# A mixer and mixture-of-experts trunk: a ninth slot for expert weights, a weight ring of ten, and a new order at the start, in the router and in the tail

## The chip, the cores and the metric

The kernel runs on one core of a Trainium2 chip. The metric is the time of one execution in microseconds (us), less is better. A core has four engines with an instruction stream each, TensorE (PE), VectorE (DVE), ScalarE (ACT) and GpSimd (POOL), and SyncE (SP), whose stream here holds almost nothing but transfers from and to memory. Each engine runs its stream in order and waits at an instruction until what it needs is done.

## The reference, cut to what matters

One layer on 256 tokens of width 2048; everything in float32.

```
mod = silu(c) @ ada_w + ada_b                     # six vectors of 2048: sh1, sc1, g1, sh2, sc2, g2
h = rmsnorm(x) * (1 + sc1) + sh1
proj = h @ mix_in_w                               # q, k, v of 16 heads, and u of 4 Fourier groups
y_na = neighborhood_attention(q, k, v, rpb) @ na_out_w
y_f = fourier_mix(u) @ fourier_out_w
g_na, g_f = split(sigmoid(h @ branch_gate_w + b))
x = x + g1 * ((g_na * y_na + g_f * y_f) @ mix_out_w)
h = rmsnorm(x) * (1 + sc2) + sh2
group = argmax(h @ router_group_w + b);  two best of its 8 experts by h @ router_expert_w + b
x = x + g2 * sum over the two of weight * (silu(h @ w_gate) * (h @ w_up)) @ w_down
out = rmsnorm(x) * final_g
```

The weights of all 32 experts are read: each has a gate and an up matrix of 2048x512 and a down matrix of 512x2048.

## The kernel before, in words

**Split products.** The projections keep float32's accuracy by splitting: a weight chunk of 128x1024 numbers (half a MB) is loaded by `load` (line 103) into a ring of eight slots, ScalarE rounds it to `hi` (line 107), VectorE takes `lo = w - hi` (line 108), and TensorE adds three products, hi with hi, hi with lo and lo with hi, into PSUM (`t_part`, `n_part`; all matmuls come from `mm`, line 116). The activations are split in the same way, into `hh` and `hl` (mixer) or `mh` and `ml`.

**Start and mixer, up to about 545 us.** c is spread over the partitions (`condR`, line 197). x comes in as two tiles of 128 tokens, `xt[0]` and `xt[1]`; ScalarE squares and sums them (line 339), VectorE scales both by 1/rms (line 342), TensorE transposes, and the eight pieces of `xT` are copied out of PSUM by VectorE and ScalarE in turn (line 350). The modulation of the first norm (sh1, sc1) comes from 64 chunks of `ada`, for which VectorE does one multiply with a sum each (`dot`, line 215). Eight such dots make the modulation `ab` of two of the sixteen 128-channel blocks of x; `h_pair` then forms `hf` (block one on VectorE, line 252, block two on ScalarE, line 253) and splits it into hh and hl. Only then can TensorE use those two blocks. The first pass over the input weights (`mixw`, `gatew`) goes by four such steps of two pairs each; in each step nine outputs take two chunks of weights. The other modulations (`ada`, 128 chunks) are macs on VectorE (line 223), one after most chunks of the mixer. A scheduler that estimates when each operand is ready sets the order of each engine's stream there.

**The stage of mow, about 545 to 641.7 us.** 4 column blocks of 512 with 8 chunks of `mix_out_w` each. `residual` (lines 600 to 602) multiplies by g1, adds to x1 and squares; `router_part` transposes x1 (line 610) and multiplies it with the router's weights (`plg`). SyncE's order is as the program text has it: beside the 32 mow chunks, 20 quarters (half a MB each) of the first five expert chunks (`early_some`, line 572) and 14 ada chunks; 9 ada chunks are loaded behind the last mow chunk (`late`), and their macs are called behind `gather(0)`.

**Transition.** The logits, with the 36 outputs on partitions, are copied (`lgs`, line 647), turned by a selector matmul and scaled to `lg` (line 656); then come the two best experts, their ranks `rk`, and `gather(0)`: selection matrices `gt`, gathered tokens `ph`, `hq`.

**The experts.** Eight quads of four experts with up to 32 tokens each. A quad reads 24 chunks `exw` of 128x4096 numbers: 16 for gate and up (`pg`, `pu`), 8 for down (`pd`, then `po` back to the tokens and a sum into x2). SyncE issues each chunk (line 727) as soon as its slot is free; there are seven slots in a ring and an eighth used once. The last quad ends with a norm and the output (`tail`, lines 886 to 918). A value `nri` that says whether a token list has over 32 entries goes to SyncE (line 869), and a loop runs only if so.

## Time and profile before

| | |
|---|---|
| median of 3 runs | 1600.57 us (1597.12 to 1603.39) |
| the profiled execution | 1598.41 us, its span 1596.6 us |
| bytes moved | 616.27 MB |
| TensorE busy | 1233.2 us, 77% of the span |
| VectorE busy | 679.3 us, 43% |
| ScalarE busy | 349.7 us, 22% |

The span runs from the first to the last instruction of the profiled execution; starts in the rows are counted from it. "Busy" counts an engine's instructions, however well they are packed. The transfers are run by 16 engines of their own, whose share and rate (GB/s) the profile gives for any stretch. PEclk is the clock that TensorE was granted, as a part of full speed.

### The profile page before, as it was taken

What the parts mean: (1) busy time and instruction counts of PE and PEld (TensorE: products, weight loads), DVE (VectorE), ACT (ScalarE), POOL (GpSimd) and SP (SyncE); (2) the same over time, 40 slices, a digit from 0 to 9 for tenths busy, and PEclk for the clock granted to TensorE, in tenths of its full rate; (3) what the DMA queues carried; (4) which work ended last, traced back from release to release, by engine and by line L of the source; (5) the groups of instructions that cost most, each with busy time, mean ns of one, the idle gap of its engine ahead of it and who ended that gap; (6) DMA issues with size and microseconds to landing.
All of it is one profiled execution on the core that took longest, in us unless ns stands there. A gap on an engine that the chain in (4) does not pass through costs nothing.

```text
span 1596.6 us, 20401 instructions
## 1 busy us (share of the span) xinstructions
PE 1233.2 (77%) x8430; PEld 745.9 (47%) x8430; DVE 679.3 (43%) x946; ACT 349.7 (22%) x535; POOL 43.6 (3%) x40
## 2 busy tenths in 40 slices
PE   4999999999999899679657567667567566556755
PEld 3989999999899777325112112112112112111111
DVE  6989999798887966603003002002002002002002
ACT  3543355444555343112000000000000000000002
POOL 0000000300002100000000000000000000000001
PEclk9999999999999999799889779789779889777878
DMA  9999999899997899699999999999999999999996
GB/s 360 389 337 339 352 359 365 273 328 369 329 346 267 318 409 380 261 427 426 427 426 427 428 427 426 427 426 427 426 427 428 427 427 426 417 427 426 425 428 280
DMA packets 89229, 616.27 MB, mean 386 GB/s; under 512 B 10037, under 2 KB 10341, under 8 KB 64937
## 3 DMA queue, kind: packets, MB, share of 16 engines
q1 hardware_dynamic: 87700, 611.10, 95.2%
q10 hardware_dynamic: 1252, 3.48, 0.6%
q8 instruction: 68, 1.11, 0.3%
q0 software_dynamic: 176, 0.31, 0.1%
q14 instruction: 33, 0.26, 0.0%
HBM read 611.71 MB, written 2.10 MB: 384 GB/s over the span
## 4 chain that ended last, share of the span: by engine, by line
DMA 47%; PE 38%; DVE 5%; issue 1%; ACT 1%; POOL 0%; DVEq 0%; POOLq 0%; ACTq 0%
DMA w<-exw 45%; PE acc L116 23%; PE pd L116 3%; PE m L116 2%; PE ph L116 2%; PE pg L116 2%; PE pu L116 2%; DMA w<-ada 2%; DVE lo L108 1%; DVE ada L223 1%; PE po L116 1%; PE at_u L116 1%; PE pr L116 0%; DVE t L600 0%; PE sp L116 0%
## 5 line engine op out<-in xcount | busy, mean ns | idle before, releaser
L116 PE MATMUL pg<-w,hq 128*32 128x512 f32 x1024 | 185.0, 777 | 217.0 <-DMA w<-exw 217.0
L108 DVE TENSOR_TENSOR lo<-w,hi 128x1024 fp32r<-128x1024 f32 x192 | 239.5, 1253 | 42.6 <-ACT hi L107 37.8
L107 ACT CAST hi<-w 128x1024 fp32r<-128x1024 f32 x192 | 200.8, 1051 | 229.2 <-PE acc L116 179.5
L790 DVE TENSOR_TENSOR act<-act,pu 128x512 f32<-128x512 f32 x8 | 5.5, 688 | 526.2 <-PE pu L116 526.2
L116 PE MATMUL acc<-hh,hi 128*128 128x256 f32 x768 | 212.1, 280 | 0.6 <-ACT hi L107 0.6
L116 PE MATMUL acc<-hl,hi 128*128 128x256 f32 x768 | 211.3, 278 | 0.0
L116 PE MATMUL acc<-hh,lo 128*128 128x256 f32 x768 | 205.7, 279 | 2.2 <-DVE lo L108 2.1
L116 PEld LDWEIGHTS pg<-w,hq 128*32 128x32 f32 x1024 | 25.0, 118 | 363.1 <-DMA w<-exw 345.3
L116 PE MATMUL pu<-w,hq 128*32 128x512 f32 x1024 | 190.0, 793 | 0.0
L223 DVE SCALAR_TENSOR_TENSOR ada<-w,condT,ada 128x1024 f32<-128x1024 f32 x124 | 162.1, 1314 | 13.1 <-DMA w<-ada 12.2
L116 PE MATMUL pd<-w,aT 128*32 128x512 f32 x1024 | 132.2, 630 | 37.0 <-DMA w<-exw 35.5
L116 PEld LDWEIGHTS acc<-hh,hi 128*128 128x128 f32 x768 | 145.3, 189 | 2.1 <-ACT hi L107 1.4
L116 PEld LDWEIGHTS acc<-hl,hi 128*128 128x128 f32 x768 | 145.1, 189 | 0.3 <-issue 0.2
L786 ACT ACTIVATE act<-pg 128x512 f32<-128x512 f32 x8 | 4.8, 597 | 637.3 <-PE pg L116 637.3
L116 PEld LDWEIGHTS acc<-hh,lo 128*128 128x128 f32 x768 | 141.2, 189 | 3.0 <-DVE lo L108 2.6
L116 PE MATMUL po<-yb,gwt 128*128 128x512 f32 (+1 forms) x132 | 75.0, 659 | 30.4 <-DVE yb L808 19.4
L116 PEld LDWEIGHTS pu<-w,hq 128*32 128x32 f32 x1024 | 43.0, 138 | 109.9 <-issue 108.2
L116 PEld LDWEIGHTS ph<-gt,x 128*128 128x128 f32 x512 | 65.2, 195 | 43.8 <-issue 25.6
L116 PEld LDWEIGHTS pd<-w,aT 128*32 128x32 f32 x1024 | 28.7, 112 | 114.7 <-issue 60.4
L215 DVE SCALAR_TENSOR_TENSOR w<-w,condR 128x1024 f32<-128x1024 f32 x64 | 77.7, 1219 | 9.1 <-ACT condR L197 7.4
L116 PE MATMUL ph<-gt,x 128*128 128x128 f32 x512 | 74.8, 288 | 7.1 <-ACT hq L756 3.5
L815 DVE TENSOR_TENSOR x<-x,po 128x512 f32<-128x512 f32 (+1 forms) x66 | 44.3, 671 | 79.8 <-PE po L116 79.8
(246 smaller groups left out, 1481.4 us busy)
## 6 DMA issues: line engine op xcount, KB each, us to landing
w<-exw SPq DMA_DIRECT2D x186, 2048.0 KB, 30.7
w<-ada SPq DMA_DIRECT2D x192, 512.0 KB, 5.8
w<-mixw SPq DMA_DIRECT2D x64, 512.0 KB, 5.6
w<-gatew SPq DMA_DIRECT2D x64, 512.0 KB, 5.4
w<-mow SPq DMA_DIRECT2D x32, 512.0 KB, 10.2
w<-exw SPq DMA_DIRECT2D x24, 512.0 KB, 10.2
w<-fow SPq DMA_DIRECT2D x16, 512.0 KB, 5.3
w<-now SPq DMA_DIRECT2D x16, 512.0 KB, 5.1
```

The lines of the kernel that those rows point to most:

```text
L107: nc.scalar.copy(hi, src)
L108: nc.vector.tensor_tensor(lo, src, hi.bitcast(F32), op=OP.subtract)
L116: return nc.tensor.matmul(ps, lhsT, rhs, start=start, stop=stop, skip_group_check=True)
L215: nc.vector.scalar_tensor_tensor(w, w, 1.0, condR[:, 1024 * kh:1024 * kh + 1024], op0=OP.mult, op1=OP.mult, accum_out=dst)
L223: nc.vector.scalar_tensor_tensor(a, w, condT[:, kc:kc + 1], a, op0=OP.mult, op1=OP.add)
L786: nc.scalar.activation(at_[:, 0], pg, AF.Silu)
L790: nc.vector.tensor_tensor(at_[:, 1], at_[:, 0], pu, op=OP.mult)
L815: nc.vector.tensor_tensor(x2[:, tb, c], base[:, tb, c], po[:, 0:n], op=OP.add)
```

## The change

- The ring of half-MB chunks has ten slots instead of eight up to the end of the gates' projections, then eight; each slot has a fixed address (`half`). Expert chunks have eight slots in the ring and a ninth used once (`NX` 8), and memory is laid out anew for it (pools `cq`, `r4`, `wq`, `tp`).
- From the end of the first pass on, SyncE's transfers stand in the order of the program text; the position biases of the attention are loaded on GpSimd's queue. x1 is loaded behind the fifth mow chunk.
- In the stage of mow all ada chunks that are left are spread over the first 28 of 32 steps. Of the 20 expert quarters 6 are issued before the last mow chunk and 14 behind it. Nothing is left for `late`.
- The router's logits are formed with the tokens on partitions, so the copies and the selector matmul go; the last square is VectorE's; the steps for the experts' weights stand behind `gather(0)`'s last eviction.
- The start: ScalarE scales xt[1] and copies all of xT; its squares stand behind all of condR; both halves of hf are ScalarE's; the first pair's dots go by halves of c; the second pair's stand behind the first hl.
- The tail: the last two chunks of weights are laid out so that 128 columns can be finished at a time, the last chunk comes in pieces of 1, 0.5 and 0.5 MB, and one output transfer is issued by ScalarE.

The diff, cut to its core:

```diff
+    def half(s):
+        p, i = rings.pop(0)
+        rings.append((p, i))
+        return p.tile([P, 1024], F32, tag=f"w{i}", bufs=1, name=nm(s))
     def load(src):
-        w = wp.tile([P, 1024], F32, tag="w", name=nm("w"))
+        w = half("w")
...
-    ada1_q = [(pr, i, u, kh) for pr in range(8) for i in range(2) for u in range(2) for kh in range(2)]
+    ada1_q = [(0, i, u, kh) for kh in range(2) for i in range(2) for u in range(2)]
+    ada1_q += [(pr, i, u, kh) for pr in range(1, 8) for i in range(2) for u in range(2) for kh in range(2)]
...
+            with tc.issue_after(h_first[0].ins) if pr == 1 else ExitStack():
+                dot(load(A["ada1"][u, 2 * pr + i, kh]), ada1_parts[pr][:, u, i, kh:kh + 1], kh)
...
-        nc.vector.tensor_scalar(hf[:, 0, :], xT[:, 2 * pr, :], ab[:, 1, 0:1], ab[:, 0, 0:1], op0=OP.mult, op1=OP.add)
-        nc.scalar.activation(hf[:, 1, :], xT[:, 2 * pr + 1, :], AF.Identity, bias=ab[:, 0, 1:2], scale=ab[:, 1, 1:2])
+        for i in range(2):
+            nc.scalar.activation(hf[:, i, :], xT[:, 2 * pr + i, :], AF.Identity, bias=ab[:, 0, i:i + 1],
+                                 scale=ab[:, 1, i:i + 1])
...
-    for tb in range(2):
-        nc.vector.tensor_scalar(xt[tb], xt[tb], rs1[:, tb:tb + 1], None, op0=OP.mult)
+    nc.vector.tensor_scalar(xt[0], xt[0], rs1[:, 0:1], None, op0=OP.mult)
+    nc.scalar.activation(xt[1], xt[1], AF.Copy, scale=rs1[:, 1:2])
...
-        (nc.scalar.copy if k2 % 2 else nc.vector.tensor_copy)(xT[:, 2 * k2:2 * k2 + 2, :], pv)
+        nc.scalar.copy(xT[:, 2 * k2:2 * k2 + 2, :], pv)
...
-                mm(plg[64 * i:64 * i + 36, 0:T], wra[:, kc, :], xt2[:, i, :], kc < 2, kc >= KC - 2)
+                for tb in range(2):
+                    mm(plg[:, 36 * tb:36 * tb + 36], xt2[:, i, tb * P:tb * P + P], wra[:, kc, :],
+                       kc == 0 and tb == 0, kc == KC - 1)
...
-                early_some(max(0, i - 5) * 4 * NA // 26 - max(0, i - 6) * 4 * NA // 26)
-                ada_some((i + 1) * PACE // 32 - i * PACE // 32)
+            ada_some(min(left, (i + 1) * left // 28) - (left - len(ada_q)))
+            if i == 4:
+                nc.sync.dma_start(x1, A["x"])
+            if i % 4 == 3 and i > 4:
+                early_some(1)
...
-            if cb == 3:
-                late = [ada_load() for _ in range(len(ada_q))]
+        if cb == 3:
+            early_some(len(quarters))
...
     hg = gather(0, rk, 1)
-    for go in late:
-        go()
+    behind, first_evict = ExitStack(), last_evict[0]
+    behind.enter_context(tc.issue_after(last_evict[0].ins))
+    nc.vector.tensor_tensor(ge, gl, gm[:, :, None].to_broadcast([P, 2, 4]), op=OP.subtract)
     nc.scalar.activation(ge, ge, AF.Exp)
...
-NW, NX, NA = 8, 7, 5
-LEAD, PACE = 3, 14
+NW, NQX, NX, NA = 8, 2, 8, 5
+LASTC = 1792
+LEAD = 3
```

What the change makes of the streams is seen at three places. The first is VectorE at the start, up to its first `hl`: `w,ap<-w,condR` are dots, `ab` the modulation, `lo` a chunk's low part. Before:

```order
L350 COPY xT<-px_168 128x512
L229 TENSOR_TENSOR ab_229<-ab_229,vecT 128x2
L230 SCALAR_TENSOR_TENSOR ab_229<-ab_229,vecT 128x2
L350 COPY xT<-px_180 128x512
L350 COPY xT<-px_192 128x512
L215 SCALAR_TENSOR_TENSOR w_309,ap_272<-w_309,condR 128x1024
L231 TENSOR_TENSOR ab_229<-ab_229,vecT 128x2
L215 SCALAR_TENSOR_TENSOR w_312,ap_272<-w_312,condR 128x1024
L252 TENSOR_SCALAR hf_234<-xT,ab_229 128x256
L108 TENSOR_TENSOR lo_245<-w_242,hi_244 128x1024
L215 SCALAR_TENSOR_TENSOR w_347,ap_272<-w_347,condR 128x1024
L108 TENSOR_TENSOR hl<-hf_234,hh 128x512
```

Now, from the scaling of xt[0] on:

```order
L354 TENSOR_SCALAR xt_92<-xt_92,rr_154 128x2048
L223 SCALAR_TENSOR_TENSOR w_235,ap_213<-w_235,condR 128x1024
L236 TENSOR_TENSOR ab_238<-ap_213 128x4
L237 TENSOR_TENSOR ab_238<-ab_238,vecT 128x2
L238 SCALAR_TENSOR_TENSOR ab_238<-ab_238,vecT 128x2
L239 TENSOR_TENSOR ab_238<-ab_238,vecT 128x2
L116 TENSOR_TENSOR lo_254<-w_251,hi_253 128x1024
L116 TENSOR_TENSOR hl<-hf_243,hh 128x512
L223 SCALAR_TENSOR_TENSOR w_282,ap_281<-w_282,condR 128x1024
L223 SCALAR_TENSOR_TENSOR w_285,ap_281<-w_285,condR 128x1024
L223 SCALAR_TENSOR_TENSOR w_318,ap_281<-w_318,condR 128x1024
L223 SCALAR_TENSOR_TENSOR w_321,ap_281<-w_321,condR 128x1024
```

The copies, one scaling and hf are gone from VectorE's stream, the first hl stands behind eight dots instead of thirteen, and four dots of the second pair come in a row behind it.

The second place is SyncE at the end of the stage of mow, from the third mow chunk from the end. Before:

```order
L103 DMA w_6989<-mow 128x1024
L572 DMA w_6297<-exw 128x1024
L103 DMA w_7008<-ada 128x1024
L103 DMA w_7011<-mow 128x1024
L572 DMA w_6297<-exw 128x1024
L103 DMA w_7030<-mow 128x1024
L572 DMA w_6297<-exw 128x1024
L103 DMA w_7049<-ada 128x1024
...
L103 DMA w_7066<-ada 128x1024
L727 DMA w_7327<-exw 128x4096
...
L869 TENSOR_LOAD nri
L727 DMA w_7357<-exw 128x4096
```

Now, from the fifth from the end:

```order
L111 DMA w_6968<-mow 128x1024
L111 DMA w_6986<-ada 128x1024
L589 DMA w_6305<-exw 128x1024
L111 DMA w_6990<-mow 128x1024
...
L111 DMA w_7066<-mow 128x1024
L589 DMA w_6305<-exw 128x1024 x2
L589 DMA w_6306<-exw 128x1024 x4
...
L589 DMA w_6308<-exw 128x1024 x4
L753 DMA w_7351<-exw 128x4096
...
L918 TENSOR_LOAD nri
L753 DMA w_7529<-exw 128x4096
```

Behind the last mow chunk there stood one quarter, nine ada chunks and three full chunks ahead of the load of nri; now 14 quarters and 14 full chunks stand there, of which the first four go to slots that no earlier expert chunk has used.

The third place is VectorE between the last mow chunk and the logits (`t` and `x` are the residual, `sst` the sum of squares). Before:

```order
L600 TENSOR_TENSOR t_7068<-acc_6869,g1r_5907 128x512
L223 SCALAR_TENSOR_TENSOR ada_5950<-w_7052,condT,ada_5950 128x1024
L600 TENSOR_TENSOR t_7072<-acc_6870,g1r_5907 128x512
L601 TENSOR_TENSOR x_6285<-x_6285,t_7068 128x512
L223 SCALAR_TENSOR_TENSOR ada_5950<-w_7054,condT,ada_5950 128x1024
L601 TENSOR_TENSOR x_6285<-x_6285,t_7072 128x512
L223 SCALAR_TENSOR_TENSOR ada_5950<-w_7056,condT,ada_5950 128x1024
...
L223 SCALAR_TENSOR_TENSOR ada_5950<-w_7066,condT,ada_5950 128x1024
L649 TENSOR_REDUCE sst<-ss_6323 128x2
L647 COPY lgs<-plg 36x256 x2
L656 SCALAR_TENSOR_TENSOR lg<-m_7123,rr_7114,cbr 128x36 x2
```

Now:

```order
L116 TENSOR_TENSOR lo_7069<-w_7066,hi_7068 128x1024
L617 TENSOR_TENSOR t_7098<-acc_6903,g1r_5919 128x512
L618 TENSOR_TENSOR x_6297<-x_6297,t_7098 128x512
L617 TENSOR_TENSOR t_7102<-acc_6904,g1r_5919 128x512
L618 TENSOR_TENSOR x_6297<-x_6297,t_7102 128x512
L620 SCALAR_TENSOR_TENSOR t_7102,ss_6334<-x_6297 128x512
L680 TENSOR_REDUCE sst<-ss_6334 128x2
L158 TENSOR_SCALAR rv_7147<-sst 128x2
...
L684 SCALAR_TENSOR_TENSOR lg<-plg,rr_7149,cbr 128x36 x2
```

The macs on ada and the copies lgs are gone from between the residual and lg; a square is added.

## Rows read from the trace of the kernel before

**Rows 1.** The page: the span, and GB/s in its 40 equal slices

```profile
span 1596.6 us, 20401 instructions
...
GB/s 360 389 337 339 352 359 365 273 328 369 329 346 267 318 409 380 261 427 426 427 426 427 428 427 426 427 426 427 426 427 428 427 427 426 417 427 426 425 428 280
```

**Rows 2.** Windows: us; busy us of each engine (instructions); PEclk, DMA share, GB/s

```profile
566.00:616.00 50.00, 48.55 (x224) 37.98 (x224) 31.53 (x31) 21.25 (x28) 0.00 (x0) 1.00 1.03 409
...
1000.00:1200.00 200.00, 131.65 (x777) 35.38 (x770) 17.88 (x40) 7.76 (x17) 0.00 (x0) 0.80 1.01 427
```

**Rows 3.** Windows of 2 us at the transition, columns as above

```profile
656.00:658.00 2.00, 0.00 (x0) 0.00 (x0) 1.79 (x13) 0.21 (x1) 0.00 (x0) 0.50 0.12 49
...
666.00:668.00 2.00, 2.00 (x11) 1.31 (x13) 0.76 (x2) 0.65 (x2) 0.00 (x0) 0.50 0.05 12
...
670.00:672.00 2.00, 2.00 (x20) 1.06 (x22) 0.41 (x1) 0.46 (x1) 0.00 (x0) 1.00 0.69 160
...
672.00:674.00 2.00, 2.00 (x20) 1.13 (x16) 0.11 (x1) 0.46 (x1) 0.00 (x0) 1.00 0.88 360
```

**Rows 4.** Timeline of SP's issues: start, length, engine, line, instruction, count

```profile
621.55 0.33 SPq L103 DMA_DIRECT2D w<-mow  x1
622.77 14.44 SPq L103 DMA_DIRECT2D w<-ada  x9
637.31 119.59 SPq L727 DMA_DIRECT2D w<-exw  x25
```

**Rows 5.** Timeline of VectorE, transition: start, length, line, tiles; in brackets idle before

```profile
641.44 1.28 DVE L223 SCALAR_TENSOR_TENSOR ada<-w,condT,ada 128x1024 f32<-128x1024 f32 x1
...
642.63 0.68 DVE L600 TENSOR_TENSOR t<-acc,g1r 128x512 f32<-128x512 f32 x1
...
645.63 7.26 DVE L223 SCALAR_TENSOR_TENSOR ada<-w,condT,ada 128x1024 f32<-128x1024 f32 x6
...
655.48 0.42 DVE L656 SCALAR_TENSOR_TENSOR lg<-m,rr,cbr 128x36 f32<-128x36 f32 x2 [0.30 <-PE m L116]
```

**Rows 6.** Timeline of TensorE at the transition

```profile
641.31 0.39 PE L116 MATMUL acc<-lo,mh 128*128 128x512 f32 x1
...
654.40 1.04 PE L116 MATMUL m<-cst,lgs 128*128 128x36 f32 x4 [5.08 <-issue]
...
668.71 1.03 PE L116 MATMUL pu<-w,hq 128*32 128x512 f32 x8
```

**Rows 7.** Timeline of VectorE at the start

```profile
21.49 2.48 DVE L342 TENSOR_SCALAR xt<-xt,rr 128x2048 f32<-128x2048 f32 x2
...
32.29 0.41 DVE L252 TENSOR_SCALAR hf<-xT,ab 128x256 f32<-128x256 f32 x1
...
48.01 0.69 DVE L108 TENSOR_TENSOR hl<-hf,hh 128x512 fp32r<-128x512 f32 x1
```

**Rows 8.** Timeline of ScalarE at the start

```profile
29.43 0.58 ACT L350 COPY xT<-px 128x512 f32<-128x512 f32 x1 [1.13 <-PE px L348]
...
32.79 0.62 ACT L107 CAST hh<-hf 128x512 fp32r<-128x512 f32 x1
```

**Rows 9.** Timeline of TensorE at the start

```profile
33.46 0.58 PE L116 MATMUL at_u<-hh,hi 128*128 128x256 f32 x1 [4.07 <-ACT hh L107]
```

**Rows 10.** Windows of 10 us, start and edges of two pairs, columns as in group 2

```profile
30.00:40.00 10.00, 6.02 (x24) 5.43 (x25) 9.86 (x16) 4.05 (x6) 0.00 (x0) 0.67 0.98 320
...
110.00:120.00 10.00, 7.88 (x41) 6.60 (x41) 9.35 (x17) 3.95 (x5) 0.00 (x0) 0.93 0.78 245
...
140.00:150.00 10.00, 7.86 (x54) 7.45 (x53) 9.27 (x17) 3.96 (x5) 0.00 (x0) 0.83 0.79 263
```

**Rows 11.** Waits of TensorE from 30 to 650 us: us, times, longest

```profile
PE acc L116 <- DVE lo L108: 6.4, 8, 2.1
```

**Rows 12.** Timeline of the tail, TensorE and VectorE

```profile
1581.12 1.05 PE L116 MATMUL pd<-w,aT 128*32 128x512 f32 x4 [0.21 <-DMA w<-exw]
...
1586.16 0.16 DVE L897 TENSOR_REDUCE sst<-ss 128x2 f32<-128x10 f32 x1 [0.60 <-ACT sq L890]
```

More of the change, by code (lines that the diff above doesn't have):

```diff
@@ L38, in const_table @@
     t[:, C_ONE:C_ONE + P] = 1
-    for j in range(2):
-        t[64 * j + np.arange(36), C_SELR + np.arange(36)] = 1
     t[:, C_IOTA:C_IOTA + 32] = np.arange(32)
@@ L380, in build @@
     _xp.close()
+    written = ExitStack()
+    written.enter_context(tc.manual_schedule(engines={nc.sync.engine}))
     def sig(dst, src, c):
@@ L535, in build @@
     _ra.close()
+    rings[:] = [r for r in rings if r[0] is wp]
+    _wq.close()
     mt, _mt = pool("mt", "right")
@@ L854, in build @@
     show("rk", rk)
+    behind.close()
     for q in range(NQ - 1):
```

212 lines of the change are left out of this document (118 added, 94 removed).

## Prediction

> **What bounds the kernel now.** I began with the page's slices of bytes [rows 1]. They show two halves. Up to about 640 us the bytes per second go up and down, and from 680 us on they stand at 417 to 428 GB/s up to the tail: there the weights of the experts, 192 chunks of 128x4096 numbers of four bytes, are the bound, each 2.097 MB / 427 GB/s = 4.91 us [rows 2]. Whatever is won ahead of that half reaches the end only if the transfers start or go on sooner, and whatever an engine saves inside it is worth nothing. Between the halves one slice falls to 261 GB/s. Windows of 2 us over it [rows 3] show the hole: 49 GB/s from 656, at most 12 in any window up to 670, then 160 and 360, then the full rate. In 656 to 674 that is (49 + 12 + 160 + 360) x 2 us = 1.16 MB, or 2.7 us' worth at 427; so 18 - 2.7 = **15.3 us of transfer are lost there**. The queue of SyncE [rows 4] says why: the last mow load goes out at 621.55, then nine ada loads and three full chunks, and the next chunk can only go out when TensorE has read a slot, at the first pu group's end, 668.71 + 1.03 = 669.74 [rows 6].
>
> The time from the last mow matmul, 641.31 + 0.39 = 641.7 [rows 6], to that release is 28.0 us. VectorE fills much of its first part: macs on the late ada loads, six of them in one run of 7.26 us [rows 5], two more between the residual's steps, and only then come the sum of squares and lg, at 655.48 [rows 5]. TensorE's selector matmuls at 654.40 [rows 6] wait behind that.
>
> Ahead of 640 us TensorE is nearly always busy; its waits for VectorE's lo at the accumulators add up to 6.4 us [rows 11]. So that half is its work plus the start and a few stalls.
>
> **The change part by part.** *The transition.* SyncE's last mow load waits, by its slot, for the same thing as before (the lo of the second of the last eight chunks), so it goes out some 20 us ahead of the last mow matmul. Behind it stood 0.5 MB + 9 x 0.52 + 3 x 2.10 = 11.5 MB; now 14 quarters and 4 chunks, 14 x 0.524 + 4 x 2.097 = 15.7 MB, with that load and up to 2 MB still under way 17 to 18 MB. At 427 this lasts 40 to 42 us, to 20 to 22 us behind the last mow matmul. The release comes sooner too. Of 655.48 + 0.42 - 641.7 = 14.2 us to lg, the residual's four steps of 0.68 [rows 5], of which the first starts before that matmul's end, and a square take about 2.5, transposes, copies and logits 3 to 4 and the chain to lg 1: 6 to 7.5, so lg is 7 to 8 us sooner (the eight macs in that stretch alone, 7.26 + 2 x 1.28, are 9.8). From lg to the release it was 13.8; the weights' steps that leave this stretch save about 1: 12.8. The release is then 19 to 20 us behind the last mow matmul, as the queue runs out. Left of the hole: 0 to 2.5 us, I take 0.5. Against this, 4.7 MB of ada no longer ride in the last 20 us, but fewer expert quarters go out earlier: left at the last mow matmul were what the queue still moved, from 641.7 to 656.2 at some 410 GB/s 5.9 MB (656.2, since 49 GB/s in 656 to 658 are 0.2 us' worth), and 184 chunks: 391.8 MB. Now at the last mow load 192 chunks less 6 quarters, 399.5 MB, and 1.5 to 2 MB under way are left, and 20.1 us later, at 427, 8.6 MB fewer: 392.4 to 392.9. That costs 1 to 2 us; I take 1 (-2 to +2, by where that load is issued). **The transition gives 15.3 - 0.5 - 1 = about 14 us**, 10 to 17.
>
> *A ninth slot, a ring of ten.* In the bound half a slot more can't raise 427. I put it at nothing; the cover is the queue, which never ran dry there [rows 2].
>
> *The start.* Before, TensorE's first projection matmul is at 33.46 [rows 9]. Both halves of x are normalised by 21.49 + 2.48 [rows 7], and copies of the transposes lie on two engines. Now the second half and all eight copies are ScalarE's. Ahead of the first matmul on ScalarE stand one normalisation (1.2 to 2 us: the lower end is VectorE's 2.48 / 2), four copies at 0.58 [rows 8], two hf at no more than a copy each, one hi at two copies' worth, and hh 0.62: 21.5 + 1.6 + 2.3 + 1.2 + 1.2 + 0.6 = 28.4, with hand-overs about 29.3. So 4 us sooner. But the second pair of chunks needs its own modulation, and that is VectorE's: its hl is at 48.01 [rows 7]. VectorE gives away a normalisation, four copies at about ScalarE's price and two hf (1.2 + 4 x 0.6 + 2 x 0.41 = 4.4 us), waits 2 to 3 us for the first hi and hh that it did not wait for, and has one dot more ahead of that hl (20 for 19; 1.3 us by the macs of its shape [rows 5]). The second pair starts where it did, within 1 us, and the first gain is waiting time in between. Bounds: -4 if it all passes through, +2 if TensorE falls to half clock in that wait.
>
> That wait is where a rule speaks against the change. At its start, in 30 to 40, TensorE is busy for 6.02 of 10 us and its granted clock means 0.67; at 140 to 150, at the edge of a pair, it is busy for 7.86 and the clock means 0.83 [rows 10]: behind a wait the lower level (1.2 GHz) returns. The Trainium skill (TensorE: Matmul & The Clock Gate, "HAM oscillation — how this bites in real kernels") says that a matmul loop whose bursts are parted by waits starts each burst cold, and advises one unbroken burst. By it the second pair would again start at the lower level, and the start would cost up to 2 us where I put 0; the trace agrees that this happens, not how often.
>
> *The later pairs.* hf on ScalarE takes 8 x 0.41 = 3.3 us [rows 7] off VectorE, which is the engine behind the stalls [rows 10, 11]: the two windows lose 2.1 us each, and 0.7 and 1.7 of clock. A part of that comes back, 0 to 5; new orders of loads can take as much. With the start I book **nothing for the mixer**, -6 to +6.
>
> *The stage of mow.* Nine macs that stood behind it now stand in it, 9 x 1.28 = 11.5 us more of VectorE in some 100. At the pairs' edges VectorE is busy for over 9.2 of 10 us [rows 10], in the stage of mow for 31.5 of 50 [rows 2]. No cost, +2 at the most.
>
> *The tail.* From the last pd matmul's end (1581.12 + 1.05) to the reduce at 1586.16 [rows 12] are 4.0 us over two pieces of 256 columns; one piece of 128 is left behind the last byte: half of it, and an output issue beside another. **-2 us**, -1 to -3.5.
>
> *Sum*: -14 + 0 - 2 = -16 us (ends about -26 and -5). The profiled run took 1598.41 us, its span 1596.6, 2 us under the median 1600.57. 1598.4 - 16 = 1582.4; on the median 1584.6. I take **1583 us**.
>
> **The rivals.** *The start passes through.* If VectorE reaches the second pair early and the ring of ten takes the stalls at the pairs' edges away, 4 + 5 us more: 1574. For it: VectorE has less to do. Against it: its dots stand ahead of the modulation as before.
>
> *Half of the hole stays.* If bytes that the mow stage held are only moved, or the release still waits on something late (the second accumulators' copies, a slot whose reader is late), 6 to 9 us of 15 are won: 1583 + 7 = 1590. For it: 14 quarters go to slots freed by other pools, each a wait in one queue in order. Against it: what they wait for is long done at that place.
>
> *The change does not do what it says.* If the first chunk's release is not sooner and the extra 4 MB go out behind it, the hole only shifts: 1598.
>
> *Slower: VectorE takes its dots in runs ahead of the lo's.* In the new order VectorE does four or five dots or macs in a row at the pairs' edges. If at each of six edges TensorE waits for five of 1.28 us = 6.4, that is 38 us, and with the 16 won 1583 + 38 = 1621. It decides from 24 us of such waits on, 4 us an edge. For it: the two edges of [rows 10] already lose 3 to 4 each. Against it: the counts of dots ahead of each edge's hl are the same or lower by two, and VectorE has 0.41 us less at each.
>
> **How the numbers follow.** Forecast 0.54, through-passing 0.18, half the hole 0.17, does not do what it says 0.05, slower 0.06. What a measurement of this kernel can tell from no change is about 0.5%, 8 us: faster is under 1592.6, slower over 1608.6. Faster: 0.54 x 0.97 + 0.18 + 0.17 x 0.7 = 0.82; same: 0.02 + 0.05 + 0.05 = 0.12; slower 0.06. For 8 in 10 the range has to leave out the slow case, the unchanged one and the two ends: 1571 to 1595.
>
> **What would show it.** Right: in 2 us windows no hole, or one of under 3 us, between the mow stage and the experts; the first full chunks go out at once behind the quarters; lg some 7 us behind the last mow matmul, the first pu group's end under 20; first projection matmul at 29 to 30 and the second pair's hl at 47 to 49; under 3 us from the last pd matmul to the reduce. Wrong: bytes under 400 GB/s for over 5 us around there, the last mow matmul over 8 us later or earlier than 641.7, or waits of TensorE for lo of over 15 us ahead of it.

## The result

The changed kernel takes 1610.30 us (median of 7 runs, 1608.55 to 1613.37) where the kernel before, timed beside it, takes 1601.73: a ratio of 1.0056 (95% interval 1.0044 to 1.0068). It is **slower by 0.56%**, about 9 us. The forecast was 1583 us, with 1571 to 1595 as its range and 0.06 for slower.

The profiled execution after has a span of 1608.3 us, 11.7 more than before. The page after, its span and the bytes in 40 slices:

```profile
span 1608.3 us, 20614 instructions
...
GB/s 383 363 342 318 330 335 342 248 358 366 272 319 364 250 348 332 379 423 427 427 427 427 427 428 426 427 428 428 427 427 427 426 428 426 427 428 426 427 426 288
```

Against [rows 1], the slice of 261 GB/s between the halves is gone, and the second half stands at 423 to 428 as before. The loss lies in the first half.

**Behind the last mow matmul it went much as predicted.** TensorE at the transition after, which answers to [rows 6]:

```profile
667.45 0.39 PE L124 MATMUL acc<-lo,mh 128*128 128x512 f32 x1
...
670.72 2.01 PE L124 MATMUL plg<-wr,x1t 128*128 128x36 f32 x16 [0.51 <-ACT x1t L636]
...
684.27 1.94 PE L124 MATMUL pg<-w,hq 128*32 128x512 f32 x8
685.98 1.13 PE L124 MATMUL pu<-w,hq 128*32 128x512 f32 x8
```

The release of the first slot comes at 685.98 + 1.13 = 687.1, 19.3 us behind the last mow matmul's end (667.84); before it was 28.0. VectorE's lg and SyncE's issues answer to [rows 5] and [rows 4]:

```profile
672.77 0.42 DVE L684 SCALAR_TENSOR_TENSOR lg<-plg,rr,cbr 128x36 f32<-128x36 f32 x2 [0.53 <-PE plg L124]
```
```profile
635.18 0.43 SPq L589 DMA_DIRECT2D w<-exw  x1
644.35 2.54 SPq L111 DMA_DIRECT2D w<-mow  x4
646.93 14.79 SPq L589 DMA_DIRECT2D w<-exw  x14
667.87 19.63 SPq L753 DMA_DIRECT2D w<-exw  x5
```

lg starts 4.9 us behind that matmul's end (13.8 before) and ends 5.3 us behind it, and the fourteen quarters and the first full chunks leave the queue one behind the other. The tail, TensorE's last pd group, answers to [rows 12]:

```profile
1594.59 1.08 PE L124 MATMUL pd<-w,aT 128*32 128x128 f32 x32
```

From its start to the end are 1608.3 - 1594.6 = 13.7 us, 1596.6 - 1581.1 = 15.5 before. From the last mow matmul's start to that group: 939.8 before, 927.1 after. So -12.7 for the transition and -1.8 for the tail: **-14.5** where the prediction had -14 and -2. In the traces of the kernels below that keep the new tail, that last part takes 13.7 to 15.2 us, so 0.3 to 1.8 less than before.

**Ahead of it 26.1 us were lost**: the last mow matmul starts at 667.45, before at 641.31. I followed the 4,032 matmuls that read a hi or lo tile, in their order on TensorE, in both traces. Worked out from their starts (us; the 193rd lies 8 weight chunks in, behind the first two pairs; the 3457th lies halfway through the now stage, in which the attention's output meets its weights `now`, and the 3841st begins the third of mow's four blocks; "rest" is from the last mow matmul's start to the end of the span):

| kernel | 193rd at | 193rd to 3457th | to 3841st | to last mow | last mow at | rest | span |
|---|---|---|---|---|---|---|---|
| before | 59.4 | 454.2 | 78.2 | 49.6 | 641.3 | 955.3 | 1596.6 |
| after | 63.4 | 465.8 | 85.6 | 52.6 | 667.5 | 940.8 | 1608.3 |
| difference | +4.0 | +11.6 | +7.4 | +3.0 | +26.1 | -14.5 | +11.7 |

The largest of these has no wait behind it: TensorE's matmuls stand further apart. The time from the start of one matmul to the start of the next is called the pitch here. A stretch before and one after, each inside an unbroken run of them:

```profile
72.06 0.28 PE L116 MATMUL acc<-hh,hi 128*128 128x256 f32 x1
72.18 0.28 PE L116 MATMUL acc<-hl,hi 128*128 128x256 f32 x1
...
73.08 0.28 PE L116 MATMUL acc<-hh,hi 128*128 128x256 f32 x1
```
```profile
72.52 0.28 PE L124 MATMUL acc<-hh,lo 128*128 128x256 f32 x1
72.64 0.28 PE L124 MATMUL acc<-hh,hi 128*128 128x256 f32 x1
...
73.59 0.40 PE L124 MATMUL acc<-hh,lo 128*128 128x256 f32 x2
```

From the first row of each to the last are nine matmuls: 1.02 / 9 = 113 ns before, 1.07 / 9 = 119 ns after. Over the whole stretch from the 193rd to the 3457th the median is 114 before and 119 after. The shapes, the clock (granted 1.00 in both) and the instructions are the same. What differs is where their operands begin. Each of these matmuls has a weight load ahead of it (PEld in the profile); the operand that is loaded is called the stationary one (hi and lo here), the other the moving one (hh, hl and their like). Worked out from the sizes of the tiles in the two kernels, since a trace shows no addresses, the moving one begins at 32 modulo 128 bytes before and at 96 after, and the stationary one at 96 in both. The change did that: six tiles left the pool cp, and its table of constants (`cst`) became 20 columns shorter.

### The profile page after: what moved, and what is told of

Same layout as the page of the kernel before. It is cut to its first block, busy times and chain, and to the rows that moved or that the text cites. A ratio compares the mean times of both kernels' runs of the same rounds, so it can differ in the third digit from the quotient of the medians.

```text
span 1608.3 us, 20614 instructions
## 1 busy us (share of the span) xinstructions
PE 1255.7 (78%) x8558; PEld 768.7 (48%) x8558; DVE 677.6 (42%) x936; ACT 357.0 (22%) x550; POOL 52.7 (3%) x49
## 3 DMA queue, kind: packets, MB, share of 16 engines
q8 instruction: 69, 1.13, 0.3%
## 4 chain that ended last, share of the span: by engine, by line
DMA 48%; PE 38%; DVE 3%; issue 1%; ACT 1%; POOL 0%; DVEq 0%; SPq 0%; ACTq 0%; POOLq 0%
DMA w<-exw 47%; PE acc L124 24%; PE m L124 3%; PE pd L124 2%; PE pg L124 2%; PE pu L124 2%; PE ph L124 2%; DVE lo L116 1%; PE po L124 1%; PE pr L124 1%; DMA w<-mow 1%; PE at_u L124 1%; DMA w<-now 0%; DVE ada L231 0%; PE plg L124 0%
## 5 line engine op out<-in xcount | busy, mean ns | idle before, releaser
L124 PE MATMUL pg<-w,hq 128*32 128x512 f32 x1024 | 188.8, 788 | 205.7 <-DMA w<-exw 205.7
L116 DVE TENSOR_TENSOR lo<-w,hi 128x1024 fp32r<-128x1024 f32 x192 | 239.0, 1251 | 54.6 <-ACT hi L115 50.3
L124 PE MATMUL pu<-w,hq 128*32 128x512 f32 x1024 | 195.4, 810 | 0.0
L231 DVE SCALAR_TENSOR_TENSOR ada<-w,condT,ada 128x1024 f32<-128x1024 f32 x124 | 165.8, 1343 | 14.6 <-DMA w<-ada 14.1
L124 PE MATMUL pd<-w,aT 128*32 128x512 f32 (+1 forms) x1120 | 129.8, 587 | 35.9 <-DMA w<-exw 34.4
L124 PE MATMUL po<-yb,gwt 128*128 128x512 f32 (+2 forms) x136 | 73.2, 628 | 30.4 <-DVE yb L826 20.0
L833 DVE TENSOR_TENSOR x<-x,po 128x512 f32<-128x512 f32 (+2 forms) x68 | 44.4, 655 | 82.7 <-PE po L124 82.7
```

Of the source, the lines that this page charges most:

```text
L116: return nc.vector.tensor_tensor(lo, src, hi.bitcast(F32), op=OP.subtract)
L124: return nc.tensor.matmul(ps, lhsT, rhs, start=start, stop=stop, skip_group_check=True)
L231: nc.vector.scalar_tensor_tensor(a, w, condT[:, kc:kc + 1], a, op0=OP.mult, op1=OP.add)
L833: nc.vector.tensor_tensor(x2[:, tb, o], base[:, tb, o], po[:, 0:n], op=OP.add)
```

## Experiments

My theory after the two traces was the pitch for most of the loss, and the order of work at the start, around the now stage and in the mow stage for the rest. The rivals: the written order of SyncE, and the ring of ten.

| run | edit | median us | ratio to before (95%) |
|---|---|---|---|
| a_l64 | after, left tiles +64 bytes | 1602.42 | 0.9998 (0.9988 to 1.0009) |
| b_l64 | before, left tiles +64 bytes | 1614.85 | 1.0078 (1.0061 to 1.0094) |
| a_128 | after, all at 0 modulo 128 | 1607.11 | 1.0035 (1.0022 to 1.0049) |
| s1 | a_l64, start of before | 1600.85 | 0.9998 (0.9983 to 1.0013) |
| s2 | a_l64, SyncE unwritten up to mow | 1612.12 | 1.0064 (1.0044 to 1.0084) |
| s3 | a_l64, no ada at mow's block edges | 1597.58 | 0.9978 (0.9964 to 0.9993) |
| s4 | a_l64, ring of eight | 1605.75 | 1.0021 (1.0009 to 1.0034) |
| c1 | s1 + s3 | 1595.18 | 0.9967 (0.9951 to 0.9982) |
| c2 | s3, SyncE unwritten up to the second gate section | 1608.62 | 1.0052 (1.0035 to 1.0068) |
| c3 | c2 + s1 | 1607.86 | 1.0048 (1.0031 to 1.0065) |
| q1 | a_l64, quarters spread over mow | 1598.93 | 0.9989 (0.9974 to 1.0004) |
| d1 | c1 + q1 | 1600.99 | 0.9989 (0.9975 to 1.0004) |
| d2 | c1, four ada moved into the attention | 1607.15 | 1.0032 (1.0017 to 1.0047) |
| d3 | d2 + q1 | 1606.96 | 1.0033 (1.0020 to 1.0046) |
| e1 | s1 + s2 + s3 + s4, on a_l64 | 1594.45 | 0.9950 (0.9935 to 0.9966) |
| e2 | e1, ring's slots under one tag | 1607.45 | 1.0038 (1.0021 to 1.0056) |

Every ratio has the kernel before timed beside it, and runs of different sessions are compared by it. The stages of the profiled executions, one execution each, worked out as above:

| kernel | 193rd at | 193rd to 3457th | to 3841st | to last mow | last mow at | rest | span |
|---|---|---|---|---|---|---|---|
| b_l64 | 61.0 | 469.4 | 78.6 | 49.6 | 658.7 | 953.7 | 1612.5 |
| a_l64 | 63.0 | 454.8 | 86.3 | 52.5 | 656.7 | 942.4 | 1599.1 |
| a_128 | 63.7 | 469.2 | 85.0 | 52.6 | 670.5 | 935.2 | 1605.6 |
| s1 | 61.7 | 454.1 | 84.9 | 52.6 | 653.3 | 942.2 | 1595.5 |
| s2 | 63.5 | 463.4 | 87.9 | 52.8 | 667.6 | 941.7 | 1609.3 |
| s3 | 62.5 | 455.2 | 85.0 | 50.2 | 653.0 | 942.6 | 1595.5 |
| s4 | 65.6 | 459.2 | 85.7 | 53.6 | 664.0 | 941.6 | 1605.6 |
| c1 | 64.5 | 457.2 | 85.6 | 50.2 | 657.4 | 941.0 | 1598.5 |
| c2 | 64.0 | 467.3 | 83.9 | 50.3 | 665.4 | 939.9 | 1605.4 |
| c3 | 62.3 | 465.0 | 85.1 | 50.2 | 662.6 | 943.4 | 1606.0 |
| q1 | 63.6 | 454.4 | 86.5 | 51.6 | 656.2 | 942.2 | 1598.4 |
| d1 | 62.6 | 456.5 | 85.9 | 52.4 | 657.4 | 944.1 | 1601.5 |
| d2 | 63.2 | 463.6 | 84.7 | 52.6 | 664.2 | 941.4 | 1605.6 |
| d3 | 65.1 | 465.0 | 85.8 | 52.4 | 668.4 | 941.7 | 1610.0 |
| e1 | 63.2 | 460.9 | 77.3 | 50.2 | 651.6 | 941.6 | 1593.2 |
| e2 | 60.0 | 465.4 | 87.4 | 50.2 | 663.0 | 944.3 | 1607.2 |

**The column "rest" settles the transition.** Without the change's back half it is 953.7 and 955.3 us, with it 935.2 to 944.3, whatever was done ahead. So 9 to 20 us were won there in each of these runs, and what was lost was lost ahead.

### The pitch

m1 times matmuls by themselves: runs of 48 with fixed operands that begin at chosen places; the rest of the model is left out.

> The disputed cost by itself: runs of matmuls of one form (stationary 128x128, moving 128x256, fp32r) on zeros, of which only the start address of an operand within 128 bytes changes (moving at 0, 32, 64, 96; stationary at 0, 32, 64, 96; then moving at 16, 48, 80, 112; then 512 columns; last, the four moving addresses again with loads, casts and subtractions beside them). Everything else of the model is left out. Address theory (the moving operand's place within 128 bytes sets the pitch): 113 ns at 32 and 119 at 96 as in the two kernels, whatever the stationary's place, and the least at 0, about 107 to 109; for 512 columns about 216 at 0 and 227 at 96; the same with the traffic beside. Rival (neighbours: the matmuls of the changed kernel are slowed by what the transfers, ScalarE and VectorE do beside them): one pitch at all addresses in the quiet part, and a longer one in the last part.

Its timeline of TensorE (mov and sta begin at 0, mova and staa at 32, movb and stab at 64, movc and stac at 96 modulo 128; wid are 512 columns wide):

```profile
33.48 5.62 PE L45 MATMUL po<-mova,stac 128*128 128x256 f32 x48
38.93 5.91 PE L45 MATMUL po<-movb,stac 128*128 128x256 f32 x48
44.67 5.91 PE L45 MATMUL po<-movc,stac 128*128 128x256 f32 x48
50.42 5.91 PE L45 MATMUL po<-mov,sta 128*128 128x256 f32 x48
...
95.94 5.61 PE L45 MATMUL po<-mov,stab 128*128 128x256 f32 x48
101.38 5.91 PE L45 MATMUL po<-mova,stab 128*128 128x256 f32 x48
...
170.64 33.76 PE L45 MATMUL po<-mov,stac 128*128 128x256 f32 x288
204.25 34.08 PE L45 MATMUL po<-mova,stac 128*128 128x256 f32 x288
238.16 34.72 PE L45 MATMUL po<-movb,stac 128*128 128x256 f32 x288
```

The next row's start less this row's, by 48, is the pitch: (38.93 - 33.48) / 48 = 113.5 ns with the moving operand at 32 and the stationary one at 96, which is the kernel before; (50.42 - 44.67) / 48 = 119.8 with both at 96, which is the kernel after. All sixteen (ns; moving 0 with stationary 96 is merged with the warm-up in its row, so it is taken from the starts of the last 48 matmuls there):

| stationary at | moving 0 | moving 32 | moving 64 | moving 96 |
|---|---|---|---|---|
| 0 | 119.8 | 117.3 | 117.9 | 118.1 |
| 32 | 120.0 | 120.0 | 117.3 | 117.9 |
| 64 | 113.3 | 119.8 | 119.8 | 117.3 |
| 96 | 116.7 | 113.5 | 119.6 | 119.8 |

So it is the two places together that count: 113 ns where the moving operand begins 64 behind the stationary one, in two of four cases, and about 120 where both begin at one place. With 512 columns and the stationary operand at 96 the pitch was 227 at 96 and 233 to 234 at 0, 32 and 64. The theory in the expectation that addresses matter stands; that the moving one's place alone sets the pitch, and that a start at 0 is the best, fall. What in the chip does this is not shown.

The last part of m1 was meant to put transfers, casts and subtractions beside the matmuls, but they had ended by then:

```profile
170.00:204.00 34.00, 34.00 (x290) 33.88 (x289) 0.00 (x0) 0.00 (x0) 0.00 (x0) 1.00 0.01 1
```

(columns: us; busy us of PE, PEld, DVE, ACT, POOL with instructions; granted clock, DMA share, GB/s). So the rival of neighbours wasn't tested as planned. What there is speaks against it: moving 0 with stationary 96 has 116.7 here, (204.25 - 170.64) / 288, and 116.7 in the first row, while transfers ran. But the same part shows that the places don't settle the pitch alone. Moving 32 with stationary 96, at 113.5 above, runs at (238.16 - 204.25) / 288 = 117.7 here, without neighbours. The kernels with these two places show both values too: by the median of each chunk's 24 matmuls, 14 of 124 chunks from the 193rd to the 3457th stand at 117 to 118 in the kernel before, 13 of 123 in a_l64 and 52 of 124 in e2, and nearly all others at 113 to 115. In the changed kernel, b_l64 and a_128 practically all stand at 118 to 120. What chooses between 113 and 118 stays open.

a_l64 puts 64 bytes into the pool ahead of the left tiles, so that they begin at 32 again; b_l64 does the same to the kernel before, whose left tiles then begin at 96; in a_128 all begin at 0.

```diff
# a_l64 (on after) and b_l64 (on before)
+    gap = cp.tile([P, 16], F32, name="gap")
+    nc.gpsimd.memset(gap, 0.0)
# a_128 (on after)
+    edge = r0.tile([P, 24], F32, name="edge")
+    nc.gpsimd.memset(edge, 0.0)
...
+    gap = cp.tile([P, 8], F32, name="gap")
+    nc.gpsimd.memset(gap, 0.0)
```

> The changed kernel with 64 bytes of padding in the pool on the left, so that hh, hl, yfh, ath and the other tiles there start at 32 modulo 128 as in the kernel before; hi, lo and the ring stay, and every engine's order stays. Address theory: the pitch of the 128x256 matmuls falls from 119 to 113 ns; with some 3,400 of them ahead of the mow stage 3,400 x 5.5 ns = 19 us less: last mow matmul at about 649 instead of 667.8, time about 1591 us, 0.6% under the kernel before. Rival (order and neighbours): pitch stays 119, time stays 1610.

> The mirror: the kernel before with 64 bytes of padding at the same place, so that hh and the others start at 96 modulo 128; every engine's order stays. Address theory: pitch from 113 to 119 ns, last mow matmul about 19 us later, about 1620 us. Rival (order and neighbours): no change, 1601.

> The changed kernel with 32 bytes of padding on the left and 96 on the right, so that all large tiles start at a multiple of 128 bytes; orders stay. Address theory: if a start at 0 is the cheapest, the 128x256 matmuls go from 119 to 107 to 109 ns (3,400 x 10 = 34 us) and those with 512 columns from 227 to 216 (about 570 x 11 = 6 us); where VectorE then sets the pace less comes through: 1570 to 1585. Rival (order and neighbours): 1610.

a_l64 came to 1602.42 where 1591 was expected: 8 us off the changed kernel, not 19. Its pitch is 113 to 114 again, and the stretch from the 193rd to the 3457th matmul is back at 454.8 us (454.2 before, 465.8 after). b_l64 is the mirror: pitch 120, that stretch 469.4, the time 12 us over the kernel before, and nothing else of its stages moved by over 2 us. Between them the two runs show that **the place of the operands alone costs 8 to 12 us**. The 19 in the expectation was too much. Summed over the pairs of neighbouring matmuls, what the pitch takes over 113 ns is 17.2 us in the changed kernel and 1.8 in a_l64, 15.4 less; but the longer gaps, where TensorE waits, add up to 5 us more in a_l64, so a third came back as waiting.

a_128 has pitch 120 and that stretch at 469.2, as the row at 0 and 0 of m1 says, so its theory fell. Its time is 3 us under the changed kernel because its rest is 935.2, the shortest of all. There the transfers of the experts' weights run faster; a_l64, then a_128:

```profile
800.00:1400.00 600.00, 395.91 (x2374) 114.30 (x2366) 67.27 (x134) 23.65 (x50) 0.00 (x0) 0.83 1.01 427
```
```profile
800.00:1400.00 600.00, 390.36 (x2387) 113.91 (x2387) 67.26 (x134) 23.64 (x50) 0.00 (x0) 0.86 1.01 430
```

At 430 in place of 427 GB/s, some 390 MB take about 6 to 7 us less. By the tiles' sizes only a_128 has all its large tiles at a multiple of 128 bytes, and of all these runs only it has this rate; one run shows it, and nothing tests the cause.

### The start

s1 takes the new start back: half of hf on VectorE, both scalings and every other copy there, the old order of ada1.

> The changed kernel with its left tiles moved 64 bytes (1602.4 us), and the new start taken back: half of hf on VectorE, both scalings and every other copy of x's transposes on VectorE, ada1 in its old order, no hold on the squares. Theory: the new start is what the fourth chunk's +2.7 us against the kernel before shows, so that the time falls by 2 to 3 us, to about 1600. Rival: the start's delay is made up in the later pairs, and the time stays within 1 us. Second rival: the start pays, and the time rises by 2 us or more.

1600.85 against 1602.42, ratios of 0.9998 both: the times don't tell it from nothing. In the profile the 193rd matmul comes at 61.7 where a_l64 has it at 63.0, but that is within the spread of single executions: the eight kernels on a_l64's places with the start of before have it at 60.0 to 65.1, the six with the new start at 62.5 to 65.6. So that the new start costs the 4.0 us of the table is not shown; undoing it gave back about 1, which isn't clear of the spread. What can be read is how the 4.0 come about in the two traces. TensorE at the second pair's first matmul, before and after, VectorE's hl after, and windows of 10 us before (one) and after (two):

```profile
48.30 0.28 PE L116 MATMUL at_u<-hh,hi 128*128 128x256 f32 x1
```
```profile
48.92 0.58 PE L124 MATMUL at_u<-hh,hi 128*128 128x256 f32 x1 [5.38 <-ACT hh L115]
```
```profile
49.53 0.69 DVE L116 TENSOR_TENSOR hl<-hf,hh 128x512 fp32r<-128x512 f32 x1
```
```profile
50.00:60.00 10.00, 10.00 (x88) 9.92 (x87) 9.24 (x13) 5.07 (x7) 0.00 (x0) 1.00 1.02 408
```
```profile
40.00:50.00 10.00, 4.25 (x32) 3.75 (x31) 8.96 (x19) 3.68 (x6) 0.00 (x0) 0.89 1.03 407
50.00:60.00 10.00, 10.00 (x67) 10.00 (x68) 8.84 (x16) 2.42 (x3) 0.00 (x0) 0.77 1.03 409
```

TensorE starts 4 us sooner (29.24), runs out of the first pair's work and waits 5.38 us for the second pair's hh, whose hl comes at 49.53, 1.5 later than before [rows 7]. The second pair starts 0.6 later. Its 96 matmuls then take 63.4 - 48.9 = 14.5 us, where before they took 59.4 - 48.3 = 11.1. The granted clock means 0.77 over 50 to 60, where the kernel before has 1.00: 0.23 x 10 = 2.3 us of work lost at the lower level (1.2 GHz), and a part of the 1.1 lost in 40 to 50; the longer pitch adds 96 x 6 ns = 0.6. Before, the lower level cost as much, 0.33 x 10 = 3.3 us in 30 to 40 [rows 10], but there it fell on the first pair, while the second wasn't ready, and TensorE came to that pair without a wait. This is the case that the Trainium skill names (TensorE: Matmul & The Clock Gate, "HAM oscillation — how this bites in real kernels"): a burst behind a wait starts cold. The trace agrees, with 0.77.

### The mow stage

s3 takes the ada products away from the block edges:

```diff
-            ada_some(min(left, (i + 1) * left // 28) - (left - len(ada_q)))
+            ada_some(1 if s and i < 28 else 0)
```

> The changed kernel with its left tiles moved 64 bytes (1602.4 us), and in the mow stage no ada product at the first step of a block and at most one in each other step. Theory: the ada product that stands ahead of the first lo on VectorE at each of the four block edges is most of the mow stage's 6 us over the kernel before (105.0 against 99.1 us from chunk 160 to 191), so that the time falls by about 4 us. Rival: the stage waits for its weights (ScalarE's hi waits 15.5 us for the w's DMA, 2.8 before), and the time stays within 1 us.

4.8 us off by the medians, 3.2 by the ratios, where about 4 was expected. VectorE at the third block's edge in a_l64, TensorE's wait behind it, and VectorE at the same edge in s3:

```profile
604.17 1.27 DVE L233 SCALAR_TENSOR_TENSOR ada<-w,condT,ada 128x1024 f32<-128x1024 f32 x1
605.36 1.22 DVE L116 TENSOR_TENSOR lo<-w,hi 128x1024 fp32r<-128x1024 f32 x1
```
```profile
606.63 0.50 PE L124 MATMUL acc<-lo,mh 128*128 128x512 f32 x1 [1.26 <-DVE lo L116]
```
```profile
602.11 0.68 DVE L619 TENSOR_TENSOR t<-acc,g1r 128x512 f32<-128x512 f32 x1
602.71 1.22 DVE L116 TENSOR_TENSOR lo<-w,hi 128x1024 fp32r<-128x1024 f32 x1
```

The ada product of 1.27 us stands ahead of the lo for which TensorE waits; without it the last half of the stage falls from 52.5 to 50.2 us (49.6 before). In c1, c2, c3, e1 and e2, which have the same edit, it is 50.2 or 50.3 too; in d1, d2 and d3, which change more in that stage or ahead of it, 52.4 to 52.6. c1 joins s1 and s3.

> The start of before and the mow stage without ada at block edges, together, on the changed kernel with its left tiles moved 64 bytes. Alone they took 1.6 and 4.8 us off 1602.4. Theory: the two stages are far apart and the gains add: about 1596. Rival: both fill the same lack of transfers and only the larger one counts: 1597 to 1598.

1595.18, which is 15 us under the changed kernel and 0.33% under the kernel before. Whether the two add isn't shown: the ratio of 0.9967 lies within the interval of s3 alone (0.9964 to 0.9993), and c1's trace has its 193rd matmul at 64.5, later than s3's.

q1 asks where the hole of the transition went. In it the quarters are issued at the rate of before (`early_some(max(0, i - 5) * 4 * NA // 26 - max(0, i - 6) * 4 * NA // 26)`).

> The changed kernel with its left tiles moved 64 bytes (1602.4 us), and the twenty quarters of expert chunks issued in the mow stage at the rate of before, not 6 in it and 14 behind the last mow load. Theory: the quarters are transfers that wait for nothing, and fill a hole wherever they stand: the two holes of 600 to 645 us (12.6 us lost at 427 GB/s) shrink by about 8 us and one of about 8 us opens again behind the last mow matmul, so that the time stays within 2 us. Rival: the holes in the mow stage cost nothing that reaches the end, and the time rises by 6 to 10 us.

Windows of 20 us (columns as above) of the kernel before, the changed one and q1:

```profile
600.00:620.00 20.00, 19.02 (x87) 14.49 (x86) 11.39 (x12) 7.72 (x12) 0.00 (x0) 1.00 1.03 409
...
660.00:680.00 20.00, 17.65 (x126) 9.68 (x126) 6.56 (x33) 2.20 (x5) 0.74 (x2) 0.79 0.47 184
```
```profile
600.00:620.00 20.00, 18.02 (x89) 14.58 (x88) 14.49 (x15) 8.29 (x11) 0.00 (x0) 1.00 0.85 333
...
640.00:660.00 20.00, 18.03 (x91) 14.67 (x90) 13.20 (x14) 9.66 (x13) 0.00 (x0) 1.00 0.76 285
```
```profile
600.00:620.00 20.00, 18.02 (x91) 14.61 (x89) 14.73 (x16) 8.62 (x12) 0.00 (x0) 1.00 1.03 409
...
640.00:660.00 20.00, 18.18 (x92) 14.81 (x92) 10.00 (x14) 6.89 (x11) 0.00 (x0) 1.00 0.50 187
```

In the changed kernel the hole is not gone, it stands in the mow stage: SyncE's head is a load that waits for a slot (nothing goes out from 635.6 to 644.35, in the rows above), with the quarters behind it. In q1 the mow stage runs at 409 and the hole is back at 640 to 660, and the time is 1.4 us lower by the ratios, within the 2 that the theory gave. A quarter fills a hole wherever it stands. That the end moves only with the time at which the first slot comes free fits q1 (last mow matmul and rest within 0.5 us of a_l64's), and no run here tests it by itself.

### SyncE's order and the ring

s2 leaves SyncE's order to the scheduler up to the mow stage (and the bias loads on SyncE); s4 has `NQX = 0`. c2 and c3 begin the written order at the second gate section.

> The changed kernel with its left tiles moved 64 bytes (1602.4 us), and SyncE's queue in the scheduler's order up to the mow stage, the bias loads on SyncE as before. Theory: the written order of SyncE is what costs the mixer between chunk 52 and chunk 160 (about 9 us of drift with the matmul pitch equal), so that the time falls by 4 to 8 us. Rival: that drift is VectorE's own order, and the time stays within 1 us.

> The changed kernel with its left tiles moved 64 bytes (1602.4 us), and the mixer's ring of x slots at eight in place of ten. Theory: the ninth and tenth slot give nothing that the time shows, and it stays within 1 us. Rival: the earlier loads that the ring lets through collide with the mow weights (ScalarE's wait of 15.5 us for them), and the time falls by 2 to 6 us. Second rival: with eight slots the mixer's loads come later, and the time rises by 2 us or more.

> The mow stage without ada at block edges, and SyncE's queue in the scheduler's order up to the second gate section and as written from there. Theory: with the scheduler's order the transfer lost at 427 GB/s was 67.0 us at 400 us against 77.9 with the written one, and the written order loses less from 480 us on (102.8 to 127.0 by 600 against 88.2 to 138.5), so that the two halves together give 1597.6 less 8 to 11 us: about 1588. Rival: what the scheduler wins early it has only borrowed from the ada loads that it leaves for later, and the time is that of the written order, 1596 to 1600.

> As the kernel with the scheduler's order up to the second gate section and no ada at block edges, and with the start of before. Theory: about 1586, 1 to 3 us under that kernel. Rival: the same as that kernel.

s2 missed its theory and its rival: without the written order the time is 10 us longer. In s4 the second rival holds: with eight slots it is 3 us longer. So on this front neither the written order nor the ring is what was lost. c2 missed its theory, 1588, and its rival, 1596 to 1600: its stretch to the 3457th matmul takes 467.3 us against 455.2 in s3, so with the scheduler's order up to the second gate section that stretch is 12 us longer. c3 took the same time as c2 within 1 us, as its rival said.

### The now stage, which stays open

From the 3457th to the 3841st matmul, the second half of the now stage and the first half of mow's, the changed kernel takes 7.4 us longer, and so do nearly all its variants. The waits of TensorE in this stretch (us, times, longest), before and then after, with the clock after in 10 us of it:

```profile
PE acc L116 <- DVE lo L108: 2.9, 4, 1.1
PE acc L116 <- POOL g L543: 1.8, 1, 1.8
```
```profile
PE acc L124 <- ACT hi L115: 5.1, 2, 2.9
PE acc L124 <- DVE lo L116: 3.8, 5, 1.3
```
```profile
539.20:549.20 10.00, 7.39 (x44) 7.02 (x45) 8.85 (x12) 3.14 (x3) 0.24 (x1) 0.83 1.01 407
```

That is 8.9 - 4.7 = 4.2 us more of waits, 0.17 x 10 = 1.7 of the lower clock behind the first wait for hi, which the kernel before does not have in this stretch, and some of the longer pitch. So the size is nearly accounted for in this trace, and the two waits for hi are what is new. SyncE and ScalarE ahead of the first of them:

```profile
516.81 0.33 SPq L111 DMA_DIRECT2D w<-now  x1
534.97 0.33 SPq L111 DMA_DIRECT2D w<-ada  x1
535.39 0.38 SPq L111 DMA_DIRECT2D w<-now  x1
```
```profile
540.18 1.04 ACT L115 CAST hi<-w 128x1024 fp32r<-128x1024 f32 x1 [6.44 <-DMA w<-now]
```

An ada load waits 18 us for its slot with the now loads behind it, and the next hi waits 6.44 us for one of those; in the kernel before no ada load waits for over 2.9 us there. d2 takes the ada products out of the first now section and puts four into the second attention; d1 and d3 spread the quarters beside.

> The start of before, no ada at block edges (together 1595.2 us), and the quarters spread over the mow stage. Theory: the quarters alone gave 1 to 3 us, since they keep the transfers going while SyncE waits for slots, so that the time is 1593 to 1595. Rival: with no ada at the edges SyncE waits less, the quarters only move the hole behind the mow stage, and the time stays within 1 us of 1595.2.

> The start of before, no ada at block edges (together 1595.2 us), and four ada products taken from the first now section and put into the second attention. Theory: the 8 us lost between the last gate section and the first mow chunk come from an ada load at the head of SyncE's queue that waits for a slot held by an ada product, with the now loads behind it; without ada there half or more comes back: 1588 to 1592. Rival: the wait is for the ring that shrinks from ten slots to eight there, and the time stays within 1.5 us of 1595.2. Second rival: the four products delay the attention on VectorE, and the time rises by 2 to 5 us.

> Both: the quarters spread, and no ada in the first now section. Theory: 1587 to 1591. Rival: 1593 to 1596, if neither helps.

d2 is 12 us slower than c1, 10 by the ratios. That is the second rival's direction at over twice its size: TensorE waits 7.0 us for one hi in the attention, behind 9.0 us in which ScalarE stood idle; what held ScalarE isn't shown. The stretch from the 3457th went from 85.6 to 84.7 only, so the theory missed, but d2 did not remove what it was meant to: an ada load still waits 17.5 us for its slot there. d1 missed both its theory and its rival: by the ratios it is 3.5 us over c1, so that what q1 gave alone isn't given on top of c1. d3, at 1606.96, missed both as well and is no different from d2.

Then I joined s1 to s4. e1 has the start, SyncE's order, the ring of eight and the place of the tiles of before, the transition and tail of the change, and no ada at block edges. In e2 the ring's slots have one tag, as before, which gives another order on SyncE and VectorE.

> As the kernel with the order of before up to the mow stage, but with the ring's eight slots as tiles with tags of their own, which gives another order on VectorE and SyncE. Theory: the order ahead of the mow stage is worth several us either way, and this one, which nothing tuned, is 3 to 10 us slower than that kernel. Rival: within 2 us of it.

> Start, SyncE's queue up to the mow stage, ring of eight slots with one tag, and place of the left tiles as in before; mow stage without ada at block edges; transition and tail of the change. Theory: the last mow matmul comes where it came before (641 us, within 5), the rest is 942 us, and the time is 1585 to 1593. Rival: the nine ada products that were moved ahead of the last mow matmul cost what the transition gains wherever they stand: 1595 to 1600.

I had them the wrong way round: e1 takes **1594.45 us, 0.50% under the kernel before and the best of all**, and e2 1607.45, which misses its theory and its rival (its last mow matmul comes at 663.0, not at 641). In e1 the stretch from the 3457th is back at 77.3 us, in e2 it takes 87.4; their code differs in one line, from which another order follows. Part of e1's gain is only moved: its stretch ahead of that takes 460.9, and the two together 538.2 against 541.1 in a_l64 and 532.4 in the kernel before. And the 18 us wait of an ada load can't be the whole cause, since e2 has none. SyncE's waits for ada products around there (us, times, longest), and TensorE's longest wait in the stretch:

```profile
SPq L111 <- DVE ada L233: 20.5, 20, 2.9
```
```profile
574.53 0.79 PE L124 MATMUL acc<-hi,mh 128*128 128x512 f32 x1 [4.61 <-ACT hi L115]
```

In e2 as in the changed kernel this wait for hi comes in the mow stage, soon after the load of x1, which the change moved behind the fifth mow chunk: there it waits 10.0 us (7.6 in the changed kernel) for GpSimd's g at the head of SyncE's queue, with mow loads behind it. In the kernel before it goes out behind the eighth and waits 4.2. No run moves x1's load back, so this stays a suspicion. The order of loads and products decides these us, and no single cause that I tried gives them back (SyncE's order in s2, the ring's size in s4, the four products in d2). Which pair of instructions it is stays open.

## Why the prediction was wrong

- **Transition, -14 and tail, -2: right.** The release at 19.3 us behind the last mow matmul's end where 19 to 20 was forecast, no hole behind the mow stage, -12.7 and -1.8. Inside the step two misses cancel, which is luck: lg ends at 5.3 where 6 to 7.5 was forecast, and from there to the release it took 13.9 where 12.8 was. One reading in it is off without harm: 392.4 to 392.9 against 391.8 MB are 1.4 to 2.6 us at 427 GB/s, not 1 to 2.
- **"The stage of mow. No cost, +2 at the most": failed.** In its second half alone the stage takes 3.0 us more (s3 gives back 2.3 of it, by the block edges). The step weighed VectorE's load over 50 us and not who stands ahead of whom at the edges. Of the 7.4 us ahead of it, from the middle of the now stage on, the prediction had nothing: there TensorE's waits are 4.2 us longer, and no experiment settles why.
- **The start, 0 (-4 to +2): +4.0 in the two traces.** The first matmul at 29.24 was as forecast, and the second pair starts 0.6 later, "within 1 us". What the term left out is the clock behind the longer wait, which took 2.3 and more; the rule beside the sum was the better forecast. That the new start costs this in the mean is not shown: s1, without it, takes the same time as a_l64.
- **"With the start I book nothing for the mixer, -6 to +6": failed, and here is most of it.** Start and mixer together cost 4.0 + 11.6 = 15.6 us. The sum had no term for the addresses, though the change says that memory is laid out anew. The matmul's pitch went from 113 to 119 ns over some 3,100 matmuls of 256 columns: 11.6 us in the stretch from the 193rd to the 3457th, of which a_l64 takes back 11.0; b_l64 and m1 show the same. The rows that I had read did not show the pitch; two neighbouring rows of TensorE in the kernel before, and the sizes of the tiles, would have raised the question, though not its sign.
- The slower rival (dots ahead of lo's at the pairs' edges, 1621) is not what happened: from the 193rd to the 3457th matmul a_l64 needs 454.8 us, before 454.2, and TensorE's waits for lo ahead of the last mow matmul add up to 12.6 us after the change, under the 15 named as a sign. Another sign came true: the last mow matmul over 8 us later than 641.7.

What the sum should have been, by the profiled spans: -14.5 behind the last mow matmul, +11.6 in the stretch where the pitch tells, +4.0 at the start, +7.4 and +3.0 in the now and mow stages: +11.7 (the rounded terms give 11.5).

## What to carry over

Where a change moves tiles, work out where the operands of the most frequent matmul begin, modulo 128 bytes, before and after, and read the pitch from two neighbouring rows: 6 ns on 3,100 matmuls took back most of what a well-sized step had won. Cut a trace by the count of matmuls, and compare the parts: a gain and a larger loss stood in two different columns here, and the total told neither. Where a scheduler orders a long stage, its order can be worth some 10 us (here 13 between e1 and e2, whose code differs in one line), so a back half that is surely better should be put on a front whose order is kept.
